# RMSNorm with repeated rows: one store cut into four transfers by partitions, and the next load held by a GpSimd copy

## The chip, the cores and the metric

The kernel runs on one core of one Trainium2 chip. The metric is the device time of one execution in microseconds (us). For the kernel before, the median of three timed runs is 238.04 us, with 237.98 and 238.66 us as the lowest and highest. The profile describes one further execution, which took 238.07 us by the same clock and has a span of 236.2 us in the trace. The difference of 1.87 us lies outside what the trace covers.

## The reference: what is computed

The input `x` has 8 x 512 = 4096 rows of 2048 float32 values, `gamma` has 2048 values. Each row is divided by its root mean square, multiplied by `gamma`, and written twice, so the output has twice as many rows as the input.

```python
x_rep = np.repeat(x, 2, axis=1)
rms = np.sqrt((x_rep ** 2).mean(axis=-1, keepdims=True) + 1e-6)
return (x_rep / rms * gamma[None, None, :]).astype(np.float32)
```

The traffic that this needs is 33.6 MB of reads and 67.1 MB of writes to the chip's memory (HBM).

## The kernel before, in words

On-chip memory (SBUF) has 128 partitions. One tile `y` (line 46) holds 24 rows of 8 KB in every partition. It is used as three regions of eight rows, and the code names their first rows: `first` is 0, `second` is 8, `third` is 16. The work comes in two groups, one for each call of `four` (lines 142 and 143). A group loads two blocks of `x` and stores four blocks of output. Every one of these twelve transfers moves 8.39 MB: 128 partitions with 64 KB each.

Inside a group the order is written out by hand (`manual_schedule`, line 84), and each engine follows it:

- Load A goes to rows 4 to 11, so it straddles `first` and `second` (line 92). Load B fills `third` (line 94).
- ScalarE (ACT in the profile) squares and sums the rows (`squares`, line 57), VectorE (DVE) multiplies them by the reciprocal root and by `gamma` (`scale`, line 70), and either of the two makes the second copy of each row (`repeat`, line 80).
- Load A gives the stores from `first` (line 99) and from `second` (line 104). Load B gives a second store from `first` (line 109) and one from `third` (line 112).

All loads of `x` and all stores are issued by SyncE (SP) on one DMA queue, q1 in the profile. SP takes its instructions in order, so an instruction that waits holds those behind it. A transfer that has been issued stands in the queue until the transfers ahead of it have been moved. The queue is served by 16 DMA engines.

What orders the transfers between the groups is the reuse of `y`. Load A of the second group overwrites rows 4 to 11, and so it waits until the stores from `first` and `second` have landed in HBM. Load B of the second group overwrites `third`, and so it waits until the last store of the first group has landed. In SP's order the last store of the first group (line 112) stands directly ahead of these two loads.

`gamma` is loaded on ScalarE's queue (q10) into partition 0: 16 pieces of 125 values (line 122), and the last 48 values in three further transfers of 16 values (line 128). GpSimd (POOL) then spreads each of the two portions over all partitions (lines 132 and 136). The landing zone lies in rows 0 to 2 of `y`, which are free at that time.

Of the kernel before, what the change touches and what calls it, by code (L numbers as in the profile page):

```python
# [1 line left out]

# [4 lines left out]


@with_exitstack
def kernel(  # L10
    ctx: ExitStack,
    tc: tile.TileContext,
    x: bass.AP,
    gamma: bass.AP,
    out: bass.AP,
):
    nc = tc.nc
    P = nc.NUM_PARTITIONS
    f32 = mybir.dt.float32
    Act = mybir.ActivationFunctionType  # L20
    Alu = mybir.AluOpType

    B, S, D = x.shape
    Bo, So, Do = out.shape
    R = So // S
    assert R == 2 and D == Do and B == Bo and So == S * R
    eps = 1e-6
    inv_d = 1.0 / float(D)


    K = 4
    N = B * S
    ntiles = N // (P * K)
    assert N % (P * K) == 0 and ntiles == 8
    H = 2
    x_t = x.rearrange("b s d -> (b s) d").rearrange("(n p k) d -> n p k d", p=P, k=H * K)
    out_t = out.rearrange("b s d -> (b s) d").rearrange("(n p h j) d -> n h p (j d)", p=P, h=H, j=K * R)

    singles = ctx.enter_context(tc.tile_pool(name="singles", bufs=1))
    rows = ctx.enter_context(tc.tile_pool(name="rows", bufs=1))  # L40
    junk = ctx.enter_context(tc.tile_pool(name="junk", bufs=1, space=bass.MemoryType.PSUM))
    small = ctx.enter_context(tc.tile_pool(name="small", bufs=4))

    y = rows.tile([P, 3 * K * R, D], f32, name="y")
    first, second, third = 0, K * R, 2 * K * R

    def load(n, at):
        nc.sync.dma_start(out=y[:, at : at + H * K, :], in_=x_t[n])  # L50

    def store(n, h, to):
        nc.sync.dma_start(
            out=out_t[n, h], in_=y[:, to : to + K * R, :].rearrange("p j d -> p (j d)")
        )

    def squares(at, rows):

        n = len(rows)
        ss = small.tile([P, n], f32, name=f"ss{n}")  # L60
        for c, k in enumerate(rows):
            sq = junk.tile([P, D], f32, name="sq")
            nc.scalar.activation(  # L63
                out=sq[:], in_=y[:, at + k, :], func=Act.Square, accum_out=ss[:, c : c + 1]
            )
        rms = small.tile([P, n], f32, name=f"rms{n}")
        nc.scalar.activation(out=rms[:], in_=ss[:], func=Act.Sqrt, scale=inv_d, bias=eps_t[:])  # L67
        return rms

    def scale(at, to, rows, rms):  # L70
        n = len(rows)
        rstd = small.tile([P, n], f32, name=f"rstd{n}")
        nc.vector.reciprocal(out=rstd[:], in_=rms[:])  # L73
        for c, k in enumerate(rows):
            nc.vector.scalar_tensor_tensor(  # L75
                out=y[:, to + R * k, :], in0=y[:, at + k, :], scalar=rstd[:, c : c + 1],
                in1=gamma_b[:], op0=Alu.mult, op1=Alu.mult,
            )

    def repeat(to, k0, k1, copy):  # L80
        y_r = y[:, to + R * k0 : to + R * k1, :].rearrange("p (k r) d -> p k r d", r=R)
        copy(out=y_r[:, :, 1, :], in_=y_r[:, :, 0, :])  # L82

    ctx.enter_context(tc.manual_schedule())

    half = K // 2
    up, down = list(range(K)), list(range(K - 1, -1, -1))

    def four(n, constants, step):


        load(n, first + K)
        constants()
        load(n + 1, third)
        for rows in (up[:half], up[half:]):
            scale(first + K, first, rows, squares(first + K, rows))
        repeat(first, 0, half, nc.scalar.copy)
        repeat(first, half, K, nc.vector.tensor_copy)
        store(n, 0, first)
        scale(second, second, down, squares(second, down))  # L100
        repeat(second, half, K, nc.scalar.copy)
        for k in range(0, half, step):
            repeat(second, k, k + step, nc.vector.tensor_copy)
        store(n, 1, second)
        roots = [squares(third + h * K, up) for h in range(H)]
        scale(third, first, up, roots[0])
        repeat(first, 0, half, nc.scalar.copy)
        repeat(first, half, K, nc.scalar.copy)
        store(n + 1, 0, first)
        scale(third + K, third, up, roots[1])  # L110
        repeat(third, 0, K, nc.scalar.copy)
        store(n + 1, 1, third)

    gamma_b = singles.tile([P, D], f32, name="gamma_b")
    G, E = 16, 3
    C = D // G - E
    gamma_s = y[0:1, 0:2, :].rearrange("p k (c d) -> p (k c) d", c=G // 2)
    gamma_t = y[0:1, 2, :]
    eps_t = singles.tile([P, 1], f32, name="eps_t")

    def constants():
        nc.scalar.dma_start(
            out=gamma_s[0:1, :, :C],
            in_=gamma[: G * C].rearrange("(p c d) -> p c d", p=1, c=G),
        )
        for c in range(E):
            at = G * C + c * G
            nc.scalar.dma_start(
                out=gamma_t[0:1, c * G : (c + 1) * G],
                in_=gamma[at : at + G].partition_broadcast(1),  # L130
            )
        nc.gpsimd.partition_broadcast(  # L132
            out_ap=gamma_b[:, : G * C].rearrange("p (c d) -> p c d", c=G),
            in_ap=gamma_s[0:1, :, :C],
        )
        nc.gpsimd.partition_broadcast(out_ap=gamma_b[:, G * C :], in_ap=gamma_t[0:1, : E * G])  # L136
        nc.vector.memset(eps_t, eps)  # L137

        root = singles.tile([P, 1], f32, name="root")[:]
        nc.scalar.activation(out=root, in_=eps_t[:], func=Act.Sqrt)  # L140

    four(0, constants, half)
    four(2, lambda: None, 1)


# [1 line left out]
_INS = ['x', 'gamma']  # L147
_OUTS = [((8, 1024, 2048), 'float32')]


# [23 lines left out]
```

## Time and profile before

| What | Value |
|---|---|
| Median of three timed runs | 238.04 us (237.98 to 238.66) |
| Profiled execution | 238.07 us, span 236.2 us |
| VectorE busy | 84.5 us (36% of the span), 48 instructions |
| ScalarE busy | 110.2 us (47%), 86 instructions |
| GpSimd busy | 2.8 us (1%), 6 instructions |
| DMA queue q1 | 100.66 MB, 98.7% of 16 engines' span |
| Mean rate over the span | 426 GB/s |
| Last store of group 1 issued, load A and load B of group 2 issued | 87.08, 100.04, 119.74 us |

The busy time of an engine is the time in which it executed instructions. The share of a DMA queue is the time that its packets took, over the time of 16 engines. "Issue" is the moment at which SP hands over a transfer, "landing" the moment at which its completion is signalled. SPq is SP's own stream of instructions.

### The profile page before, as it was taken

To read this page: it belongs to the slowest core of one execution; us is meant where nothing else is said; L and a number is where in the kernel's file an instruction comes from. 1 tells how busy PE (TensorE), PEld (TensorE's weight loads), DVE (VectorE), ACT (ScalarE), POOL (GpSimd) and SP (SyncE) were. 2 spreads that over 40 slices of the span, in tenths; PEclk is the share of its full clock that TensorE was granted. 3 is DMA by queue.
4 is the path that set the end of the run, shared out by engine and by line. 5 is a ranking of instruction groups with operands and counts; after the bars stand their busy time and mean duration, and the time that the engine had idled before them with its cause. 6 is when DMAs were issued, how large, how long until landed. Compare 5 with 4: busy or idle time off the path is not lost.

```text
span 236.2 us, 226 instructions
## 1 busy us (share of the span) xinstructions
DVE 84.5 (36%) x48; ACT 110.2 (47%) x86; POOL 2.8 (1%) x6
## 2 busy tenths in 40 slices
DVE  0000396594699500000000007928919992000000
ACT  2001989479998470000000049991999957400000
POOL 0110000000000000000000000000000000000000
DMA  9898989989898989989898998989898998989894
GB/s 355 356 533 355 510 377 422 466 366 522 355 533 356 533 355 422 466 377 510 355 533 355 488 400 355 533 355 533 355 533 355 488 399 355 533 355 533 355 533 178
DMA packets 1767, 100.68 MB, mean 426 GB/s; under 512 B 230, under 2 KB 230, under 8 KB 230
## 3 DMA queue, kind: packets, MB, share of 16 engines
q1 hardware_dynamic: 1728, 100.66, 98.7%
q10 hardware_dynamic: 38, 0.01, 0.0%
q14 instruction: 1, 0.01, 0.0%
HBM read 33.56 MB, written 67.11 MB: 426 GB/s over the span
## 4 chain that ended last, share of the span: by engine, by line
DMA 45%; ACT 26%; DVE 12%; issue 2%; DVEq 0%
DMA y<-in_x_dram 26%; DMA out_dram<-y 20%; ACT sq L63 15%; DVE y L75 12%; ACT y L82 11%; ACT rms L67 1%; DVE rstd L73 0%; DVEq L75 0%
## 5 line engine op out<-in xcount | busy, mean ns | idle before, releaser
L63 ACT ACTIVATE sq<-y 128x2048 f32<-128x2048 f32 x32 | 60.1, 1878 | 71.1 <-DMA y<-in_x_dram 70.4
L75 DVE SCALAR_TENSOR_TENSOR y<-y,rstd,gamma_b 128x2048 f32<-128x2048 f32 x32 | 73.8, 2349 | 1.6 <-DMA out_dram<-y 1.0
L82 ACT COPY y<-y 128x4096 f32<-128x4096 f32 (+1 forms) x10 | 42.6, 4283 | 19.1 <-DVE y L75 18.3
L73 DVE RECIPROCAL rstd<-rms 128x4 f32<-128x4 f32 (+1 forms) x10 | 1.7, 170 | 109.2 <-ACT rms L67 109.2
L82 DVE COPY y<-y 128x4096 f32<-128x4096 f32 (+1 forms) x5 | 9.2, 1865 | 0.1
L63 ACT ACTIVATION_READ_ACCUMULATOR sq<-y 128x1 f32 x32 | 6.0, 186 | 0.0
L67 ACT ACTIVATE rms<-ss,eps_t 128x4 f32<-128x4 f32 (+1 forms) x10 | 3.0, 297 | 0.3
L140 ACT ACT_TABLE_LOAD x1 | 1.3, 1283 | 2.6 <-issue 2.6
L132 POOL PARTITION_BROADCAST gamma_b<-y x1 | 2.2, 2243 | 10.2 <-DMA y<-in_gamma_dram 10.2
L136 POOL PARTITION_BROADCAST gamma_b<-y x1 | 0.3, 323 | 10.1 <-DMA y<-in_gamma_dram 10.1
L137 DVE MEMSET eps_t<- 128x1 f32 x1 | 0.1, 59 | 0.8 <-PEq L158 0.8
L140 ACT ACTIVATE root<-eps_t 128x1 f32<-128x1 f32 x1 | 0.2, 203 | 0.0
L158 POOL MEMSET const-bfloat16-1.0<- 128x1 bf16 x1 | 0.1, 102 | 0.0
L158 POOL MEMSET const-float32-0.0<- 128x1 f32 x1 | 0.1, 99 | 0.2 <-issue 0.2
L158 POOL MEMSET const-uint8-127<- 128x1 uint8 x1 | 0.1, 101 | 0.0
L158 POOL MEMSET const-float32-1.0<- 128x1 f32 x1 | 0.1, 98 | 0.0
## 6 DMA issues: line engine op xcount, KB each, us to landing
out_dram<-y SPq DMA_DIRECT2D x8, 24.8
y<-in_x_dram SPq DMA_DIRECT2D x4, 31.4
y<-in_gamma_dram ACTq DMA_DIRECT2D x3, 0.1 KB
y<-in_gamma_dram ACTq DMA_DIRECT2D x1, 7.8 KB, 9.8
```

The source lines that it names most:

```text
L63: nc.scalar.activation(out=sq[:], in_=y[:, at + k, :], func=Act.Square, accum_out=ss[:, c : c + 1])
L67: nc.scalar.activation(out=rms[:], in_=ss[:], func=Act.Sqrt, scale=inv_d, bias=eps_t[:])
L73: nc.vector.reciprocal(out=rstd[:], in_=rms[:])
L75: nc.vector.scalar_tensor_tensor(out=y[:, to + R * k, :], in0=y[:, at + k, :], scalar=rstd[:, c : c + 1], in1=gamma_b[:], op0=Alu.mult, op ...
L82: copy(out=y_r[:, :, 1, :], in_=y_r[:, :, 0, :])
L132: nc.gpsimd.partition_broadcast(out_ap=gamma_b[:, : G * C].rearrange("p (c d) -> p c d", c=G), in_ap=gamma_s[0:1, :, :C],)
L136: nc.gpsimd.partition_broadcast(out_ap=gamma_b[:, G * C :], in_ap=gamma_t[0:1, : E * G])
L137: nc.vector.memset(eps_t, eps)
L140: nc.scalar.activation(out=root, in_=eps_t[:], func=Act.Sqrt)
L158: nc = _bacc.Bacc("TRN2", target_bir_lowering=False, num_devices=1)
```

## The change

Three things are changed, and one detail with them.

1. `store` gets a list of slices of partitions and issues one transfer for each. The last store of the first group (from `third`) is issued as four transfers: the odd partitions (64 of them), partitions 2, 6, 10, ... (32), partitions 0, 8, 16, ... (16), and partitions 4, 12, 20, ... (16). All other stores stay one transfer.
2. Between the groups, GpSimd copies one element of partition 0: from row 4, which load A of the second group overwrites, to row 16, the first row of `third`. The third of the four transfers reads row 16 of partition 0, so the copy waits until that transfer has landed. Load A overwrites what the copy reads, so load A waits for the copy.
3. `gamma` comes in one transfer of 16 pieces of 128 values, with one spreading instruction.
4. The argument `step` is gone: in the second group, VectorE makes the repeat of the two rows of `second` in one instruction instead of two.

```diff
-    def store(n, h, to):
-        nc.sync.dma_start(
-            out=out_t[n, h], in_=y[:, to : to + K * R, :].rearrange("p j d -> p (j d)")
-        )
+    def store(n, h, to, parts=(slice(None),)):
+        rows = y[:, to : to + K * R, :].rearrange("p j d -> p (j d)")
+        for part in parts:
+            nc.sync.dma_start(out=out_t[n, h][part], in_=rows[part])
...
-    def four(n, constants, step):
+    def four(n, constants, parts=(slice(None),)):
...
-        for k in range(0, half, step):
-            repeat(second, k, k + step, nc.vector.tensor_copy)
+        repeat(second, 0, half, nc.vector.tensor_copy)
...
-        store(n + 1, 1, third)
+        store(n + 1, 1, third, parts)
...
-    G, E = 16, 3
-    C = D // G - E
+    G = 16
+    C = D // G
...
         nc.scalar.dma_start(
-            out=gamma_s[0:1, :, :C],
-            in_=gamma[: G * C].rearrange("(p c d) -> p c d", p=1, c=G),
+            out=gamma_s[0:1, :, :C], in_=gamma.rearrange("(p c d) -> p c d", p=1, c=G)
         )
-        for c in range(E):
-            at = G * C + c * G
-            nc.scalar.dma_start(
-                out=gamma_t[0:1, c * G : (c + 1) * G],
-                in_=gamma[at : at + G].partition_broadcast(1),
-            )
...
-        nc.gpsimd.partition_broadcast(out_ap=gamma_b[:, G * C :], in_ap=gamma_t[0:1, : E * G])
...
-    four(0, constants, half)
-    four(2, lambda: None, 1)
+    odd, even, last = slice(1, P, 2), slice(2, P, 4), slice(4, P, 8)
+    four(0, constants, (odd, even, slice(0, P, 8), last))
+    nc.gpsimd.tensor_copy(out=y[0:1, third, 0:1], in_=y[0:1, first + K, 0:1])
+    four(2, lambda: None)
```

More of the change, by code (lines that the diff above doesn't have):

```diff
@@ L111, in four @@
         repeat(third, 0, K, nc.scalar.copy)
-        store(n + 1, 1, third)
+        store(n + 1, 1, third, parts)
     gamma_b = singles.tile([P, D], f32, name="gamma_b")
-    G, E = 16, 3
-    C = D // G - E
+    G = 16
+    C = D // G
     gamma_s = y[0:1, 0:2, :].rearrange("p k (c d) -> p (k c) d", c=G // 2)
-    gamma_t = y[0:1, 2, :]
     eps_t = singles.tile([P, 1], f32, name="eps_t")
@@ L122, in constants @@
         nc.scalar.dma_start(
-            out=gamma_s[0:1, :, :C],
-            in_=gamma[: G * C].rearrange("(p c d) -> p c d", p=1, c=G),
-        )
-        for c in range(E):
-            at = G * C + c * G
-            nc.scalar.dma_start(
-                out=gamma_t[0:1, c * G : (c + 1) * G],
-                in_=gamma[at : at + G].partition_broadcast(1),
-            )
+            out=gamma_s[0:1, :, :C], in_=gamma.rearrange("(p c d) -> p c d", p=1, c=G)
+        )
         nc.gpsimd.partition_broadcast(
-            out_ap=gamma_b[:, : G * C].rearrange("p (c d) -> p c d", c=G),
-            in_ap=gamma_s[0:1, :, :C],
+            out_ap=gamma_b[:].rearrange("p (c d) -> p c d", c=G), in_ap=gamma_s[0:1, :, :C]
         )
-        nc.gpsimd.partition_broadcast(out_ap=gamma_b[:, G * C :], in_ap=gamma_t[0:1, : E * G])
         nc.vector.memset(eps_t, eps)
```

## The prediction

> **What bounds the kernel now.** I read the page from the top: busy shares, the 40 slices, the DMA queues, the chain that ended last. Then SP's instructions in order of time, and a table by stage.
>
> ```profile
> span 236.2 us, 226 instructions
> DVE 84.5 (36%) x48; ACT 110.2 (47%) x86; POOL 2.8 (1%) x6
> DMA  9898989989898989989898998989898998989894
> DMA packets 1767, 100.68 MB, mean 426 GB/s; under 512 B 230, under 2 KB 230, under 8 KB 230
> q1 hardware_dynamic: 1728, 100.66, 98.7%
> ```
>
> No compute engine is busy half of the time, and the DMA row never falls under 8 before the last slice. q1 carries twelve equal transfers, so one takes 236.2 x 0.987 / 12 = 19.43 us, and an eighth of one (16 partitions with 64 KB each) 2.43 us.
>
> ```profile
> 0.72 21.92 DMA y<-in_x_dram
> 76.17 23.86 DMA out_dram<-y
> 100.04 38.78 DMA y<-in_x_dram
> 155.30 22.23 DMA out_dram<-y
> ```
>
> In this view (the chain that ended last: start, length, what) the long pieces are transfers. The compute pieces between them do not stop the queue, as the table by stage says (stretch, length, busy time of DVE, ACT and POOL, clock, DMA share, GB/s):
>
> ```profile
> 2.00:80.00 78.00, 42.18 (x23) 48.81 (x43) 2.57 (x2) 1.00 0.98 425
> 80.00:120.00 40.00, 0.01 (x1) 7.02 (x1) 0.00 (x0) 1.00 1.01 436
> 120.00:200.00 80.00, 42.25 (x24) 51.11 (x42) 0.00 (x0) 1.00 1.00 433
> ```
>
> The change acts in the second stretch, which is the fullest of all. What keeps it full is seen in SP's issues:
>
> ```profile
> 87.08 0.33 SPq L53 DMA_DIRECT2D out_dram<-y  x1
> 100.04 0.34 SPq L50 DMA_DIRECT2D y<-in_x_dram  x1
> 119.74 0.34 SPq L50 DMA_DIRECT2D y<-in_x_dram  x1
> ```
>
> Load A of group 2 is issued at 100.04, when the store ahead of the last one has landed. The whole last store, 19.43 us of work, then still stands in the queue. That store lands 19.70 us later, which lets load B go at 119.74, with the whole of load A as cover. Each wait of SP is hidden under one full transfer.
>
> **The change part by part.**
>
> *Load A waits for the third part.* The parts are an eighth times 4, 2, 1 and 1. In the built program load A waits for GpSimd's copy, and the copy for the third part, not the fourth. So load A is issued with only the fourth part, 2.43 us, left as cover, instead of 19.43 us. The steps between the end of the third part and load A's data:
> - Landing to GpSimd: the gamma transfer was issued at 0.73 and landed 9.8 us later, at 10.53; GpSimd began at 10.65. 0.12 us.
> - The copy. No copy on GpSimd is in the trace. The nearest rows are below, the memsets with 0.10 us and the spreading of 48 columns with 0.32 us; I take 0.20 for one element.
> - GpSimd to SP: VectorE's repeat ends at 36.83 + 2.29 = 39.12, SP issues the store at 39.20. 0.08 us.
> - Issue to data. The only load into an empty queue is the first: 21.92 us from issue to use, 2.49 us more than the 19.43 that its bytes take. Its two issues took 0.86 us together, 0.43 each against 0.34 at 100.04, so 2.40 to 2.49 us; I take 2.45. The signal of landing is in this figure, and the third part's own signal comes just as late after its bytes, so it need not be added a second time.
>
> ```profile
> 0.33 0.10 POOL L158 MEMSET const-uint8-127<- 128x1 uint8 x1
> 10.65 2.24 POOL L132 PARTITION_BROADCAST gamma_b<-y  x1 [10.22 <-DMA y<-in_gamma_dram]
> 23.01 0.32 POOL L136 PARTITION_BROADCAST gamma_b<-y  x1 [10.12 <-DMA y<-in_gamma_dram]
> ```
>
> Sum: 0.12 + 0.20 + 0.08 + 2.45 = 2.85 us against a cover of 2.43: the queue runs dry for 0.42 us. With the small ends it is 0.27, with the large ones 0.58. The far ends: a copy as dear as the costliest GpSimd row (2.24) makes it 2.50 us. On the other side, the transfer ahead of the queued load took 19.70 us from landing to landing, 0.27 more than the mean. If the load that stands queued behind it is the cause, holding that load back wins up to 0.27 us. I take 0.42, since its rows are of the same kinds of step.
>
> Behind the waiting copy GpSimd has nothing. Behind load A on SP stand load B and the stores of group 2. Load B still needs all four parts landed, about 2.4 us after load A goes, and has load A's 19.43 us as cover. After that each step of group 2 moves by the gap.
>
> *The four transfers.* Three more issues of about 0.34 us on SP at 87 to 88.5: the store ahead of them lands only at 100.04, so they are hidden by some 11 us. If that backlog were gone, they would cost 1.0 us. Tiny packets: q1 has 144 packets for 128 rows in each transfer, so 16 more for each added transfer, 48 in all. All 192 of now fit, with the start and the end, into the 1.3% (3.1 us) that q1 is not busy, so 48 cost between 0 and 0.1 us; I take 0.03.
>
> *The speed of the parts.* The trace has no large transfer from some of the partitions only. The nearest rows are the full stores, 2.43 us for 16 rows of 64 KB on 16 engines; I take that for every part. The dear end: if the 16 rows of a small part are served by half of the engines, or two engines share one way, they take two turns, 4.86 us. If the same held for all four parts, the store would take 38.9 us.
>
> [...]
>
> *Gamma.* Three small transfers and one spreading instruction go, the large one spreads 2048 columns instead of 2000 (about 2.30 us). Now the second spreading ends at 23.33, and VectorE first uses gamma at 27.34: 4 us of slack before, more after. The issues on ACT go too (1.21 us), but ACT's first square waits for load A until 22.67. Worth 0; if they had disturbed the first load, at most 0.05.
>
> *VectorE's repeat in group 2.* Two copies of 1.18 us become one of 2.29, 0.07 less. The store that waits for it is issued at 172.02. Stores take 22.2 to 32.6 us to land for 19.43 of work, so at least 2.8 us of queue stand ahead of any. Worth 0.
>
> Sum against the profiled execution: 238.07 + 0.42 + 0.03 = 238.52; the median stands 0.03 lower, so **238.5 us**.
>
> **The rivals.**
> - *The gap is hidden.* [...] For it: 100.04 to 119.74 has room for 0.27 us of gain. Against it: the first load shows the whole 2.49. Between 237.8 and 238.1 us.
> - *The small parts don't run as one row per engine* (slower). Place: third and fourth part. If each takes two turns, the cost is 2 x 2.43 = 4.86 us, less what the longer cover hides of the gap (all of it): 242.9. If the two run side by side on different halves of the engines, no bytes are late, but the third lands with the fourth and the cover is gone: 2.85 us, 240.9. It decides as soon as a part needs a second turn. For it: nothing but the unusual shape; against it: the steady 436 GB/s of full transfers, which is not the same shape.
> - *All four parts at half speed*: 19.43 us more, 257.5.
> - *GpSimd's copy is slow to start*, its first ordinary instruction after the spreading. By the dearest GpSimd row 240.6. [...]
> - *The change doesn't do what it says*: the copy could be released early, if its wait were already met. Then nothing is lost, 238.1. The built program's wait on the third part's own counter speaks against it; I count it with the first rival.
>
> **How the numbers follow.** Chances: gap of about 0.45 us 0.45 (its own range 237.9 to 239.2, as a median of this kernel moves by some 0.3 either way), hidden 0.12, small parts in two turns or late 0.21, all parts slow 0.13, slow copy 0.09. About 0.3%, 0.71 us, is what a measurement of this kernel can tell from no change (its three runs lie 0.68 apart). Within it: two thirds of the first case (0.31) and most of the second (0.08), 0.39. Faster: 0.04, from the second, since the queue was never idle and no bytes go away. Slower: 0.14 + 0.21 + 0.13 + 0.09 = 0.57. The likeliest single case is the first, though the slower ones together weigh more. The range 237.8 to 243.0 leaves out the case of all parts slow (0.13) and the edges of the others.
>
> **What would show it.** Right: the third part lands an eighth before 119.74, at 117.31; GpSimd's copy starts at 117.4 and lasts under 0.4 us, SP issues load A at about 117.7 instead of 100.04 and load B near 119.8; one DMA slice near 118 a little emptier; the second group as before, all about 0.45 us later. Wrong on the parts: the interval from 100.04 to load B's issue grows from 19.7 to 22, 24 or 39 us, with GB/s in that stretch well under 436. Wrong on the copy: GpSimd waits for the landing, and load A's issue follows by microseconds. Faster: load A's first bytes without a dip, and a store tail under 19.4 us.

## The result

The changed kernel takes 244.45 us (median of six runs, 243.73 to 244.97), the kernel before beside it 238.18 us. The ratio is 1.0261, with a 95% interval of 1.0241 to 1.0281: 2.6% slower, some 6.3 us. That is above the range of the forecast (237.8 to 243.0). Gamma, the four parts and the hold of load A all act in it; the profile shows where most of the time went.

The head of the page of the kernel after:

```profile
span 242.7 us, 229 instructions
DVE 84.4 (35%) x47; ACT 110.2 (45%) x86; POOL 2.7 (1%) x6
DMA  8999999999998989899699999998989898989894
GB/s 346 401 464 400 464 443 421 454 410 464 400 475 389 486 378 497 367 508 356 173 324 443 421 443 421 443 412 378 497 367 497 367 508 356 508 378 486 378 486 184
q1 hardware_dynamic: 1776, 100.66, 98.1%
```

The span is 6.5 us longer, and the compute engines did the same work in it. One slice of the GB/s row stands out: 173, the twentieth of forty, from 115 to 121 us. The same row of the kernel before has 355 there:

```profile
GB/s 355 356 533 355 510 377 422 466 366 522 355 533 356 533 355 422 466 377 510 355 533 355 488 400 355 533 355 533 355 533 355 488 399 355 533 355 533 355 533 178
```

The DMA row of the kernel after has a 6 in that slice, its only digit under 8 ahead of the last slice. In these views a packet counts where it starts, so short stretches swing, and their DMA share can pass 1.

SP's issues, and the copy on GpSimd (from the views of SP's and GpSimd's instructions in order of time):

```profile
87.10 0.57 SPq L55 DMA_DIRECT2D out_dram<-y  x1
89.14 2.81 SPq L55 DMA_DIRECT2D out_dram<-y  x2
119.23 0.35 SPq L50 DMA_DIRECT2D y<-in_x_dram  x1
123.42 0.34 SPq L50 DMA_DIRECT2D y<-in_x_dram  x1
119.03 0.17 POOL L133 COPY y<-y 1x1 f32<-1x1 f32 x1 [106.20 <-DMA out_dram<-y]
```

Load A is issued at 119.23, where the forecast had 117.7, and load B at 123.42, where it had 119.8. The copy itself took 0.17 us, and SP followed 0.03 us after its end: those steps were sized well. What came late was the landing of the third part. From 100.04 to load B's issue are 23.4 us, and a growth from 19.7 to 22, 24 or 39 was the forecast's own sign of slow parts.

The table by stage shows why (stretch, length, busy time of DVE, ACT and POOL, clock, DMA share, GB/s). The kernel before, in the stretch of the small parts and load A's first rows:

```profile
100.00:113.50 13.50, 0.00 (x0) 0.00 (x0) 0.00 (x0) 1.00 0.91 393
113.50:122.50 9.00, 0.00 (x0) 0.00 (x0) 0.00 (x0) 1.00 1.08 459
122.50:128.00 5.50, 0.00 (x0) 0.00 (x0) 0.00 (x0) 1.00 0.88 381
```

And the kernel after:

```profile
100.00:113.50 13.50, 0.00 (x0) 0.00 (x0) 0.00 (x0) 1.00 0.92 393
113.50:122.50 9.00, 0.00 (x0) 0.00 (x0) 0.17 (x1) 1.00 1.04 269
122.50:128.00 5.50, 0.00 (x0) 0.00 (x0) 0.00 (x0) 1.00 0.89 298
```

Up to 113.5, which is where the odd partitions and the 32 partitions 2, 6, 10, ... are moved, the two kernels run alike. Then the rate falls from 459 to 269 GB/s while the DMA share is still 1.04 (1.08 before). The engines were mostly not idle, they were slow. The packets in the trace say the same: a row of 64 KB takes 2.42 us on its engine, but each of the 16 rows of the third part took 4.16 to 4.69 us, side by side on 16 engines, and those of the fourth 3.40 to 4.84.

From the packet records one can follow the end of the slowest of the 16 engines, row by row (the kernel before has no parts; its rows are those at the same place in the store):

| End of a row on the slowest engine, us | before | after | four parts, no hold |
|---|---|---|---|
| second part (last row) | 114.07 | 114.12 | 114.01 |
| third part | 116.49 | 118.57 | 118.40 |
| fourth part | 119.03 | 123.01 | 124.49 |
| first row of load A | 121.45 | 128.02 | 126.91 |
| last row of the kernel | 235.01 | 241.52 | 240.40 |

The kernel after is 6.57 us late after load A's first row and 6.51 late at the end. On this measure all of the loss arises between 114 and 128 us and nothing of it comes back. The last column belongs to the first experiment.

### The profile page after: what moved, and what is told of

Same layout as the page of the kernel before. It is cut to its first block, busy times and chain, and to the rows that moved or that the text cites. A ratio compares the mean times of both kernels' runs of the same rounds, so it can differ in the third digit from the quotient of the medians.

```text
span 242.7 us, 229 instructions
## 1 busy us (share of the span) xinstructions
DVE 84.4 (35%) x47; ACT 110.2 (45%) x86; POOL 2.7 (1%) x6
## 3 DMA queue, kind: packets, MB, share of 16 engines
q1 hardware_dynamic: 1776, 100.66, 98.1%
## 4 chain that ended last, share of the span: by engine, by line
DMA 50%; DVE 22%; ACT 12%; issue 1%; SPq 1%; POOLq 0%; DVEq 0%
DMA out_dram<-y 31%; DVE y L75 20%; DMA y<-in_x_dram 20%; ACT y L82 7%; ACT sq L63 5%; DVE y L82 1%; SPq L55 1%; DVE rstd L73 0%; ACT rms L67 0%; POOLq L160 0%; DVEq L75 0%; POOLq L133 0%
## 5 line engine op out<-in xcount | busy, mean ns | idle before, releaser
L82 DVE COPY y<-y 128x4096 f32<-128x4096 f32 x4 | 9.2, 2293 | 0.1
```

## The experiments

The theory after the result, called P: a part's rate goes by which partitions it takes, and the loss is that of the third and the fourth part, with rows of 4.16 to 4.69 and 3.40 to 4.84 us in place of 2.42; the rest is as forecast. Why partitions 0, 8, 16, ... and 4, 12, 20, ... are slow is not shown by the trace. Rivals: H, the hold of load A empties the queue and is the loss; S, small or widely strided parts are slow by themselves; and, for the small edits, that they are not free. All times given as measured are medians; beside each experiment the kernel before was timed on the same chip.

**The four parts without the hold.**

```diff
-    nc.gpsimd.tensor_copy(out=y[0:1, third, 0:1], in_=y[0:1, first + K, 0:1])
```

> The four parts of the last store stay, the copy on GpSimd goes, so load A is issued as early as before the change. [...] Rival H (the loss comes from holding load A back, which empties the queue): 238.2 to 238.6 us, and no part over 2.6 us.

Measured: 243.87 us, ratio 1.0244 (1.0229 to 1.0259). Its table by stage:

```profile
100.00:113.50 13.50, 0.00 (x0) 0.00 (x0) 0.00 (x0) 1.00 0.90 388
113.50:122.50 9.00, 0.00 (x0) 0.00 (x0) 0.00 (x0) 1.00 1.10 291
122.50:128.00 5.50, 0.00 (x0) 0.00 (x0) 0.00 (x0) 1.00 1.00 381
```

Load A stands in the queue all the time, and still the stretch of the small parts moves 291 GB/s at a DMA share of 1.10. H falls: most of the loss is there with no hold at all. The third part's rows took 4.07 to 4.67 us. Two parts with rows of 4.5 us in place of 2.42 would by estimate add 4.2 us; the total is 5.8 over the kernel before, partly because gamma's edit is in it too (below).

**The same sizes, other partitions, with the hold.** The last two parts become the 32 partitions 0, 4, 8, ... cut by columns; `store` takes pairs of slices for it, partitions and columns (not shown):

```diff
-    odd, even, last = slice(1, P, 2), slice(2, P, 4), slice(4, P, 8)
-    four(0, constants, (odd, even, slice(0, P, 8), last))
+    odd, even, rest = slice(1, P, 2), slice(2, P, 4), slice(0, P, 4)
+    W = K * R * D // 2
+    four(0, constants, (odd, even, (rest, slice(0, W)), (rest, slice(W, 2 * W))))
```

> The hold stays. The last two parts are no longer 16 partitions each, but the same 32 partitions (0, 4, 8, ...) twice, first the left half of their columns, then the right half; each part still moves 1.05 MB. [...] Rival S (small transfers with a wide stride of partitions are slow by themselves): each part still takes about 4.5 us, 243 to 244.5 us. Rival H: about 244 us, as the hold is unchanged.

Measured: 238.99 us, ratio 1.0040 (1.0025 to 1.0055). Table by stage, GpSimd's copy and SP's issue of the loads:

```profile
113.50:122.50 9.00, 0.00 (x0) 0.00 (x0) 0.17 (x1) 1.00 1.13 462
116.99 0.17 POOL L135 COPY y<-y 1x1 f32<-1x1 f32 x1 [104.05 <-DMA out_dram<-y]
117.19 2.50 SPq L50 DMA_DIRECT2D y<-in_x_dram  x2
```

Same bytes in each part, same hold, same cover: 462 GB/s, and 5.5 us less than the changed kernel. S and H fall together. With parts of full speed the steps come within 0.5 us of the forecast (117.4 for the copy, 117.7 for the issue, measured 116.99 and 117.19).

**The whole store in one transfer, load A held until it has landed.**

```diff
-    four(0, constants, (odd, even, slice(0, P, 8), last))
+    four(0, constants)
     nc.gpsimd.tensor_copy(out=y[0:1, third, 0:1], in_=y[0:1, first + K, 0:1])
```

> The last store is one transfer again, and load A is still held by the copy, now until that whole store has landed. This measures the price of a hold with no cover. Theory P with the forecast's own sum of steps: 2.85 us over before, 241.0 us, up to 242 if the first rows of the load start cold. Rival H: at least as long as the changed kernel, 244.5 us or more, since the queue empties completely.

Measured: 241.48 us, ratio 1.0147 (1.0130 to 1.0164). The chain that ended last:

```profile
86.95 32.20 DMA out_dram<-y
119.50 21.82 DMA y<-in_x_dram
```

Load A starts into an empty queue and takes 21.82 us from issue to use, against 19.43 for its bytes: 2.39, where the forecast's bounds were 2.40 to 2.49. Against the kernel with only the small edits (next, 238.70) this hold costs 2.78 us; the forecast's sum of the steps was 2.85. So the price of a hold was right, and even a hold with no cover at all costs less than half of the 6.3 us.

**The small edits alone**: gamma in one transfer and the merged repeat, no parts, no hold.

```diff
-    four(0, constants, (odd, even, slice(0, P, 8), last))
-    nc.gpsimd.tensor_copy(out=y[0:1, third, 0:1], in_=y[0:1, first + K, 0:1])
+    four(0, constants)
```

> Only gamma in one transfer and VectorE's single repeat in group 2; the last store is whole and load A isn't held. Theory P: no change, 238.0 to 238.4 us. Rival: if the gamma edit disturbed the first load, it would show here as 238.6 us or more.

Measured: 238.70 us against 238.06, ratio 1.0029 (1.0015 to 1.0042). The edits costed at nothing are not free. The first load is not what they disturb: it took 21.79 us from issue to use here, 21.92 before. Two other things are in the trace. First, an 8 KB transfer on the instruction queue (q14) lies at 75.0 us in the kernel before and at 152.5 us here. The view of the DMA queues for 74.9 to 75.4 us, kernel before:

```profile
q14 instruction: 1, 0.01, 3.9%
```

and the same line for 152.4 to 152.9 us in this one:

```profile
q14 instruction: 1, 0.01, 3.9%
```

Right after it one row on one engine takes 2.72 us instead of 2.42 (2.54 in the kernel before). In the kernel before the ends of the 16 engines lie 0.62 us apart ahead of the fetch and behind it, and they draw together to 0.33 us at the change from stores to loads near 119 us. Here the fetch comes behind that, and the slowest engine ends at 235.26 instead of 235.01, while the mean over the engines is the same (234.82 and 234.81). Second, with three transfers fewer the last store signals on another counter, and at the end SP works through three more waits after it, 0.06 us each.

**Three parts, none small, a quarter as cover.**

```diff
-    four(0, constants, (odd, even, slice(0, P, 8), last))
+    four(0, constants, (odd, slice(0, P, 4), even))
```

> The last store goes in three parts, each of which has rows in every group of four partitions that it touches: the odd partitions (64), then 0, 4, 8, ... (32), then 2, 6, 10, ... (32). The copy waits for the second part, so load A is held with a quarter of a store, 4.86 us, as cover. Gamma as in the change. Theory P: no part is slow, and 4.86 us is more than the 2.85 us of the steps, so nothing is lost against gamma alone (238.7): 238.6 to 238.9 us. Rival S (parts with a stride of four partitions are slow): over 240 us.

Measured: 238.51 us against 238.23, ratio 1.0013 (1.0005 to 1.0022). Nothing is lost over the small edits. Parts with a stride of four are not slow (against S), and a cover of 4.86 us is enough for the steps of 2.85.

**Two halves of 64 neighbouring partitions, no hold.**

```diff
-    four(0, constants, (odd, even, slice(0, P, 8), last))
-    nc.gpsimd.tensor_copy(out=y[0:1, third, 0:1], in_=y[0:1, first + K, 0:1])
+    four(0, constants, (slice(0, P // 2), slice(P // 2, P)))
```

> The last store goes in two parts of 64 neighbouring partitions each, 0 to 63 and 64 to 127, with no hold; gamma as in the change. The odd partitions of the change are 64 as well and ran at full rate. [...] Rival S (small or widely strided parts are slow): these are large and dense, 238.7 us.

Measured: 260.26 us, ratio 1.0924 (1.0908 to 1.0939). The table by stage:

```profile
80.00:99.00 19.00, 0.00 (x0) 7.02 (x1) 0.00 (x0) 1.00 0.95 410
99.00:138.00 39.00, 0.00 (x0) 0.00 (x0) 0.00 (x0) 1.00 1.00 213
```

213 GB/s at a DMA share of 1.00, for 39 us, against 436 GB/s at 1.01 in the kernel before: both halves run at half rate, and S, which had 238.7, falls. The 64 odd partitions of the changed kernel, the same number, ran at full rate (393 GB/s in the stretch to 113.5, as before). This is the sharpest contrast of the study: large transfers of 4.19 MB, and only the choice of partitions differs.

**Eight parts of 16 neighbours, no hold.**

```diff
-    four(0, constants, (odd, even, slice(0, P, 8), last))
-    nc.gpsimd.tensor_copy(out=y[0:1, third, 0:1], in_=y[0:1, first + K, 0:1])
+    four(0, constants, [slice(i, i + 16) for i in range(0, P, 16)])
```

> The last store in eight parts of 16 neighbouring partitions (0 to 15, 16 to 31, ...), no hold, gamma as in the change. A part has as many rows and bytes as the third part of the change. [...] Rival S (it is the small part with 16 partitions, wherever they lie): 4.5 to 5.1 us each, 238.7 + 17 to 22, 256 to 260 us.

Measured: 276.76 us, ratio 1.1619 (1.1597 to 1.1640). The 256 to 260 us of S were missed. In the packets, the 16 rows of the first part took 8.86 to 9.62 us each, about four times 2.42, and twice as long as the same number of rows from 0, 8, 16, ... (4.16 to 4.69). Eight such parts in turn would by estimate take 77 us (8 x 9.62), but the store didn't take that long, as the time grew by only 38.1 us over the small edits alone (238.70): after the first two parts the engines fall out of step, some are already in a later part with other partitions, and those rows take 2.4 to 9.7 us. The rate of one part does not give the sum over parts in one queue.

**Which of the small edits.** ScalarE padded with 16 tiny square roots, on top of the small edits:

```diff
-        nc.scalar.activation(out=root, in_=eps_t[:], func=Act.Sqrt)
+        for _ in range(1 + 16):
+            nc.scalar.activation(out=root, in_=eps_t[:], func=Act.Sqrt)
```

> Gamma as in the change, whole store, no hold, and 16 more tiny square roots on ScalarE while it waits for the first load. The edit to gamma alone cost 0.64 us. Theory F: gamma's edit takes instructions off ScalarE, and so moves an 8 KB fetch of instructions on the DMA engines from 75 us (ahead of the change from stores to loads, where the engines fall into step again) to 152.5 us (behind it), where one engine stays 0.3 us late to the end. More instructions bring the fetch forward again: 238.0 to 238.2 us. Rival G (gamma's transfer itself disturbs the first load): unchanged, 238.7 us.

Measured: 238.92 us (238.42 to 239.33) against 238.23, ratio 1.0032 (1.0020 to 1.0044). The fetch went back to 75.0 us as expected, and in the profiled execution the slowest engine ended at 235.07. That execution took 238.42, 0.27 less than the profiled one with the fetch at 152.5, but the other six took up to 239.33, so the median didn't fall. That the number of ScalarE's instructions places the fetch is shown; that the fetch is what gamma's edit costs is not.

Gamma's edit alone (the repeat stays in two instructions):

> Gamma in one transfer and nothing else: VectorE's repeat in group 2 stays in two instructions. With the run below it splits the 0.64 us that the two small edits cost together. Theory F (fewer instructions on ScalarE move the 8 KB fetch of instructions behind the first group): the fetch near 152.5 us and one engine 0.25 us late to the end, and three waits of SP behind the last store's instead of none (0.06 us each), as three transfers fewer put the last store on another counter: 238.5 to 238.7 us. Rival R (the merged repeat is the cause): 238.06 us.

Measured: 238.97 us against 238.13, ratio 1.0036 (1.0023 to 1.0049), with the fetch at 152.5; that is a little over the 238.5 to 238.7 expected.

The merged repeat alone:

> Only VectorE's repeat in group 2 in one instruction; gamma as before. Theory F: the fetch stays near 75 us, 238.06 us. Rival R: 238.5 to 238.7 us.

Measured: 238.39 us, ratio 1.0009 (1.0000 to 1.0017), with the fetch at 74.9. So most of the small edits' cost is gamma's; the 0.26 us of the repeat reach just to the edge of the interval. How much of gamma's cost is the fetch, how much SP's last waits (0.19 us) and how much lies outside the trace stays open.

**The hold on the kernel before**, with its own gamma, and the parts that run at full speed:

```diff
-    four(0, constants, half)
+    odd, even, rest = slice(1, P, 2), slice(2, P, 4), slice(0, P, 4)
+    W = K * R * D // 2
+    four(0, constants, half, (odd, even, (rest, slice(0, W)), (rest, slice(W, 2 * W))))
+    nc.gpsimd.tensor_copy(out=y[0:1, third, 0:1], in_=y[0:1, first + K, 0:1])
```

> The kernel before, with its gamma and repeats as they were, and the last store in four parts of which the last two are the 32 partitions 0, 4, 8, ... cut by columns, and load A held by the copy until the third has landed. This is the hold with an eighth as cover and no slow part. Theory P: the difference between the same parts with the new gamma (238.99) and the new gamma alone (238.70) is the gap, 0.3 us, so 238.3 to 238.5 us. Rival: if the hold costs nothing and the 0.3 came from elsewhere, 238.06 us.

Measured: 239.49 us against 238.23, ratio 1.0056 (1.0044 to 1.0068): 1.26 us, more than the 0.3 expected. Load A was issued at 117.43, 0.24 later than with the new gamma, and took 22.31 us from issue to use. By the medians an eighth of a store as cover is therefore short by 0.3 to 1.3 us, and these two runs don't say which. In the packets of the profiled executions the 16 engines end on average 0.35 us later with the new gamma (than with the small edits alone) and 0.67 us later with the old one (than in the kernel before), on either side of the 0.42 of the forecast.

**The hold with a quarter as cover, on the kernel before** (parts odd, 0, 4, 8, ..., then 2, 6, 10, ...):

> The kernel before with its own gamma and repeats, the last store in three parts (odd partitions, then 0, 4, 8, ..., then 2, 6, 10, ...) and load A held until the second has landed, with a quarter of a store as cover. Theory P with the forecast's sum of 2.85 us for the steps: covered by 4.86 us, nothing lost, 238.1 to 238.3 us. Rival: the hold costs by itself, also with cover, as much as with an eighth: 238.5 us or more.

Measured: 238.15 us against 238.13, ratio 1.0000 (0.9991 to 1.0009). GpSimd's copy and SP's issue:

```profile
114.85 0.17 POOL L145 COPY y<-y 1x1 f32<-1x1 f32 x1 [91.64 <-DMA out_dram<-y]
115.05 5.13 SPq L50 DMA_DIRECT2D y<-in_x_dram  x2
```

Load A goes 15 us later than in the kernel before, the store is in three parts, and the time is the same. It also wins nothing. No version in this study beats the kernel before.

## Why the prediction was wrong

**The bound was right.** The queue of the 16 DMA engines sets the time; what slowed it showed up whole at the end (6.57 us late after load A's first row, 6.51 at the end), and what left it full (the quarter as cover) cost nothing (238.15 against 238.13).

**The step that failed: "the speed of the parts".** It took 2.43 us for every part, from the rows of full stores, and named two turns, 4.86 us, as the dear end. The third and fourth part came near the dear end: rows of 4.16 to 4.69 us in the third and of 3.40 to 4.84 in the fourth, in place of 2.42. The four parts cost 5.17 us against the small edits alone (243.87 less 238.70). That the choice of partitions is the cause is shown: in the same kernel 64 and 32 strided partitions ran at full rate (393 GB/s up to 113.5 us, as before); with the same sizes on other partitions the loss vanished (238.99 us); 64 neighbours ran at half rate (213 GB/s), and 16 neighbours at a quarter in their first part (8.86 to 9.62 us a row). Where the limit lies is not shown: in all runs a partition's row also has its fixed place in HBM, and no run moved one without the other.

The trace before had no large transfer from some of the partitions only, so the 2.43 us for every part was an untested assumption, and the 0.21 against it was the author's estimate, drawn from no row.

**The rival was right in kind, and short.** "Small parts in two turns" gave 242.9. It let the longer fourth part hide the whole gap. In the table above the hold costs on top: with the parts and no hold, the slowest engine ends load A's first row at 126.91, with the hold at 128.02. The medians say 0.6 us for the hold (244.45 less 243.87), from two measurements whose ratios overlap. Nor did the rival count that the engines leave the slow parts out of step (from 121.44 to 123.01 us, 1.57 apart, against 0.33 in the kernel before), and that the load's first rows take longer than 2.42 us: 2.45 to 3.64 in the changed kernel, and about 3 us on many engines also without the hold. (The first rows of the kernel's very first load, into an idle queue, take 2.83 to 3.52 us too.)

**The hold's steps were right.** 0.12 us to GpSimd, 0.17 for the copy (0.20 taken), 0.03 to SP (0.08 taken), 2.39 from issue to data (2.45 taken). With no cover the sum of 2.85 was measured as 2.78. With an eighth as cover, the forecast gap of 0.42 was 0.29 with the new gamma and 1.26 with the old one, both with other small effects in them; its size stays uncertain, its sign does not.

**The slow copy fell.** GpSimd's first plain copy after the spreading showed no start-up: the landing (118.91), the copy (119.03) and SP's issue (119.23) follow in 0.3 us. The copy took 0.17 us, against the 2.24 of the dearest row.

**Gamma, "worth 0", was wrong by 0.6 to 0.8 us**, as measured without the four parts. The slack of 4 us at its first use was there and was not the point. What the edit changed was the number of instructions and transfers, and with them a fetch of instructions and the last waits; which of these costs the time stays open. **The merged repeat** was costed right within what can be told, 238.39 against 238.13, though not for the reason given: the 22.2 us of the shortest store do not show 2.8 us of queue ahead of it, since the first load, into an empty queue, took 21.92. **The added issues** were sized too small, 0.57 to 1.39 us each where 0.34 was taken, at no cost, as all ended 8 us ahead of the landing at 100 us. The tiny packets were counted right: q1 has 1776 packets in place of 1728.

By these runs the 6.3 us are about 5.2 for the four parts, two of them near half rate, 0.6 for the small edits and 0.4 to 0.6 for the hold. The share of the small edits in the full change was not measured by itself, and may be smaller there, since the count of transfers is that of the kernel before and SP has no extra waits at the end (the span ends 1.19 us after the last row, 1.22 in the kernel before).

## What to carry to other kernels

When a full-width transfer is cut by partitions, check for each piece which partitions it takes, not only how many: here strides of 2 and 4 over all 128 kept the full rate (393 GB/s, as before), a stride of 8 nearly halved it (rows of 4.16 to 4.69 us in the third part, for 2.42), 64 neighbours halved it (213 GB/s), and cutting the 32 partitions 0, 4, 8, ... by columns kept it (462 GB/s). A load may be held back as late as its steps allow (2.8 us here, from the landing to steady data) if the transfer still ahead of it is clearly longer than that (4.86 us was enough); in the full queue here, holding it won nothing (238.15 us against 238.13). In a kernel bound by one queue, a part of the estimate that rests on "same as the full transfer" deserves the widest range.

## What the runs showed that was not expected

- A DMA engine can be fully busy and move half: 213 GB/s at a share of 1.00, against 436 at 1.01 in the kernel before. The share of busy engines does not show this loss, GB/s does.
- Eight parts, the first of them at a quarter of the rate (8.86 to 9.62 us a row), cost 38 us, not the 58 that eight such parts in turn would by estimate (77 less 19.4): behind the first two the engines were out of step, with rows of 2.4 to 9.7 us.
- An 8 KB instruction fetch in the middle of the kernel moved with the number of ScalarE's instructions (75.0 us with 16 instructions added, 152.5 without), and at 152.5 the row behind it took 0.3 us longer on one DMA engine (2.72 for 2.42).
- In the changed kernel, issues of partial stores directly behind one another took SP 1.37 to 1.39 us each from the second on, against 0.33 to 0.35 for a store that stands alone.
